# Batched matmul, 32 x (512 x 1024) x (1024 x 768): two outputs per store, the store moved behind the next x, and the first x cut into more pieces

## Chip, cores, metric

One core of one Trainium2 chip. The metric is device time of the slowest (here the only) core in microseconds, lower is better. A profiled execution is shown where traces are read; its span is some 1.5 to 2 us shorter than the time.

## The reference

```python
def setup_inputs():
    batch, m, k, n = 32, 512, 1024, 768
    return {"x": randn(batch, m, k).astype(float32), "weight": randn(batch, k, n).astype(float32)}

def reference(x, weight):
    return np.matmul(x, weight).astype(np.float32)
```

100.7 MB of weights, 67.1 MB of x and 50.3 MB of output pass between HBM and SBUF once each.

## The kernel before

The loads are issued by POOL and cast to bf16 on the way. x comes in pairs of batches (except the first and last), is transposed on PE, copied by DVE, multiplied against the weight, and evacuated by ACT and DVE to a float32 output tile.

```python
    AHEAD = 3; LATE = 4; HELD = 3
    w_pool   = ...tile_pool(name="w", bufs=4)
    x_pool   = ...tile_pool(name="x", bufs=3)
    out_pool = ...tile_pool(name="out", bufs=7)
    ...
    def load_pair(b):
        xs[b] = x_pool.tile([P, 2 * MT, K], BF16, name="x_sb")
        nc.gpsimd.dma_start(out=xs[b], in_=pair_view[b // 2])
    ...
    def evacuate(b, pair, pm):
        o = outs[b][:, pair * N2:(pair + 1) * N2]
        nc.scalar.copy(o[:, 0:512], pm[0])
        nc.vector.tensor_copy(o[:, 512:1024], pm[1])
        nc.scalar.copy(o[:, 1024:N2], pm[2])
    ...
        # first x: three of its four row tiles at once, the fourth in pieces
        x_fourth = out_pool.tile([P, 1, K], F32, name="out_sb")
        nc.sync.dma_start(x_first, x_view[0, :, :MT - 1])
        few = [slice(at, first + 20, 4) for first in (0, 20, 40) for at in range(first, first + 4)]
        for rows in (slice(64, P), slice(60, 64), *few):          # 64 rows, 4 rows, 12 times 5 rows
            nc.sync.dma_start(x_fourth[rows, 0], x_view[0, rows, MT - 1])
        load_w(0); ...; load_pair(1); load_w(1); load_w(2); load_pair(3)

        for b in range(B):
            if b % 2 and b + AHEAD + 1 < B:
                ...load_pair(b + AHEAD + 1)                       # (load_last for the last one)
            if b + AHEAD < B:
                load_w(b + AHEAD)
            if b <= B - LATE:
                if b > 0:
                    pending.append(b - 1)
                if b % 2 == 0 and b + AHEAD < B - HELD or b == B - LATE:
                    for at in pending:
                        nc.gpsimd.dma_start(out=out_view[at], in_=outs[at])
                    pending = []
            ...                                                   # the last four batches leave from SP
            outs[b] = out_pool.tile([P, MT * N], F32, name="out_sb")
            ...                                                   # transposes, matmuls, evacuate
```

Of the kernel before, what the change touches and what calls it, by code (L numbers as in the profile page):

```python
# [8 lines left out]
F32 = mybir.dt.float32  # L9
# [4 lines left out]
def kernel(  # L14
# [6 lines left out]
    nc = tc.nc  # L21
    B, M, K = x.shape
    _, _, N = weight.shape
    P = 128
    MT = M // P
# [4 lines left out]
    AHEAD = 3  # L30
    LATE = 4
    HELD = 3
# [2 lines left out]
    w_pool = ctx.enter_context(tc.tile_pool(name="w", bufs=4))  # L35
    x_pool = ctx.enter_context(tc.tile_pool(name="x", bufs=3))
    xT_pool = ctx.enter_context(tc.tile_pool(name="xT", bufs=6))
    out_pool = ctx.enter_context(tc.tile_pool(name="out", bufs=7))
    tpsum = ctx.enter_context(tc.tile_pool(name="tpsum", bufs=2, space=bass.MemoryType.PSUM))
    mpsum = ctx.enter_context(tc.tile_pool(name="mpsum", bufs=2, space=bass.MemoryType.PSUM))  # L40

# [4 lines left out]
    x_view = x.rearrange("b (mi mo) k -> b mi mo k", mi=P)  # L46
    pair_view = x[1:B - 1].rearrange("(p r) (mi mo) k -> p (r mi) mo k", r=2, mo=2 * MT)
    out_view = out.rearrange("b (mi mo) n -> b mi (mo n)", mi=P)

    xs, ws, outs = {}, {}, {}  # L50

    def banks():
        return [mpsum.tile([P, 512], F32, name=f"pm{i}") for i in range(3)]
# [6 lines that stand above are left out]
    def load_last():  # L60
        xs[B - 1] = x_pool.tile([P, MT, K], BF16, name="x_sb")
        nc.gpsimd.dma_start(out=xs[B - 1], in_=x_view[B - 1])  # L62

    def load_w(b):
        ws[b] = w_pool.tile([P, KT, N], BF16, name="w_sb")
        at = 0
        for n in CHUNKED.get(b, (KT,)):
            nc.gpsimd.dma_start(out=ws[b][:, at:at + n, :], in_=w_view[b, :, at:at + n, :])  # L68
            at += n
# [9 lines left out]
    def transpose_pair(b, mt):  # L79

        both = xT_pool.tile([P, 2, JT, P // 2, 2, 2], BF16, name="xT")
        for half in range(2):
            nc.vector.tensor_copy(  # L83
                both[:, :, :, :, half, :].rearrange("p b j i r -> p j b i r"),
                words(b, mt + MT * half).rearrange("p j (b i r) -> p j b i r", b=2, r=2),
            )
        return [both[:, r].rearrange("p j i h r -> p j (i h) r") for r in range(2)]

    def transpose_last(mt):
        xT = xT_pool.tile([P, JT, P, 2], BF16, name="xT")  # L90
        nc.vector.tensor_copy(  # L91
            xT.rearrange("p j m r -> p (j m r)"), words(B - 1, mt).rearrange("p j m -> p (j m)")
        )
        return xT

    def transpose_first(mt):

        xT = xT_pool.tile([P, JT, P, 2], BF16, name="xT")
        rows = x_first[:, mt] if mt < MT - 1 else x_fourth[:, 0]
        for h in range(2):  # L100
            pt = tpsum.tile([P, JT, P], F32, name="pt")
            for i in range(JT):
                nc.tensor.transpose(pt[:, i, :], rows[:, JT * h + i::KT], ident)  # L103
            nc.vector.tensor_copy(  # L104
                xT[:, 2 * h:2 * h + 2].rearrange("p j m r -> p j r m"),
                pt.rearrange("p (j r) m -> p j r m", r=2),
            )
        return xT
# [8 lines left out]
    def matmuls(pm, half, xT, b, kos, together):  # L117
        for ko in kos:
            for i, (bank, at, off, size) in enumerate(SPLITS[half]):
                shares = half == 1 and i == 0  # L120
                nc.tensor.matmul(  # L121
                    pm[bank][:, at:at + size],
                    xT[:, ko // 2, :, ko % 2],
                    ws[b][:, ko, off:off + size],
                    start=(ko == 0 and not (together and shares)),
                    stop=(ko == KT - 1),
                    skip_group_check=together,
                )

    def evacuate(b, pair, pm):  # L130
        o = outs[b][:, pair * N2:(pair + 1) * N2]
        nc.scalar.copy(o[:, 0:512], pm[0])  # L132
        nc.vector.tensor_copy(o[:, 512:1024], pm[1])  # L133
        nc.scalar.copy(o[:, 1024:N2], pm[2])  # L134

    with tc.manual_schedule():

        x_first = x_pool.tile([P, MT - 1, K], F32, name="x_sb")
        x_fourth = out_pool.tile([P, 1, K], F32, name="out_sb")
        nc.sync.dma_start(x_first, x_view[0, :, :MT - 1])  # L140
        few = [slice(at, first + 20, 4) for first in (0, 20, 40) for at in range(first, first + 4)]
        for rows in (slice(64, P), slice(60, 64), *few):
            nc.sync.dma_start(x_fourth[rows, 0], x_view[0, rows, MT - 1])
        load_w(0)
        ident = const.tile([P, P], F32)
        make_identity(nc, ident)
        load_pair(1)
        load_w(1)
        load_w(2)
        load_pair(3)  # L150

        ready = {}
        pending = []
        for b in range(B):
            if b % 2 and b + AHEAD + 1 < B:
                if b + AHEAD + 1 == B - 1:
                    load_last()
                else:
                    load_pair(b + AHEAD + 1)
            if b + AHEAD < B:  # L160
                load_w(b + AHEAD)
            if b <= B - LATE:
                if b > 0:
                    pending.append(b - 1)
                if b % 2 == 0 and b + AHEAD < B - HELD or b == B - LATE:
                    for at in pending:
                        nc.gpsimd.dma_start(out=out_view[at], in_=outs[at])  # L167
                    pending = []
            if b == B - 1:
                halves = [slice(pair * N2, (pair + 1) * N2) for pair in range(2)]  # L170
                nc.sync.dma_start(out_view[b - 1, :, halves[0]], outs[b - 1][:, halves[0]])
                for late in range(B - LATE, B - 2):
                    nc.sync.dma_start(out_view[late], outs[late])
                nc.sync.dma_start(out_view[b - 1, :, halves[1]], outs[b - 1][:, halves[1]])
            outs[b] = out_pool.tile([P, MT * N], F32, name="out_sb")
            if b == 0:
                xT = {mt: transpose_first(mt) for mt in range(MT - 1)}
            elif b == B - 1:
                xT = {mt: transpose_last(mt) for mt in range(MT)}
            else:  # L180
                if b % 2:
                    for mt in range(MT):
                        ready[b, mt], ready[b + 1, mt] = transpose_pair(b, mt)
                xT = {mt: ready.pop((b, mt)) for mt in range(MT)}
            if b not in CHUNKED:
                for pair in range(2):
                    pm = banks()
                    for half in range(2):
                        mt = 2 * pair + half
                        if mt not in xT:  # L190
                            xT[mt] = transpose_first(mt)
                        matmuls(pm, half, xT[mt], b, range(KT), False)
                    evacuate(b, pair, pm)
                continue
            pms = [banks() for _ in range(2)]
            at = 0
            for n in CHUNKED[b]:
                last = at + n == KT
                for mt in range(MT):
                    matmuls(pms[mt // 2], mt % 2, xT[mt], b, range(at, at + n), True)  # L200
                    if last and mt % 2 == 1:
                        pair = mt // 2
                        evacuate(b, pair, pms[pair])
                        if b == B - 1:
                            nc.sync.dma_start(out_view[b, :, halves[pair]], outs[b][:, halves[pair]])
                at += n
# [30 lines left out]
```

## Time and profile before

| | before |
|---|---|
| time, median of 3 runs | 515.02 us (515.02 to 515.08) |
| span of the profiled run | 513.6 us (a run of 515.37 us) |
| stores from POOL | 28 of 1536 KB |
| transfers that POOL issues per round of two batches | 5 |

A *round* below is two batches: one pair of x, two weights, two outputs. "Transfer engines" are the 16 DMA engines of the core. For each large transfer the trace has 16 landings, one per engine, without the engine's number; their spread shows how far the engines have drifted apart. These landings were read from the packed traces directly, so no printed view shows them. The *end* of a transfer is the 4-byte packet that each engine adds after its data (1296 on POOL's queue before, 16 for each of its 81 transfers).

### The profile page before, as it was taken

Reading aid. Unit: us, or ns where it says so; the run is one execution under the profiler, and the core shown is the slowest. Engines: PE = TensorE matmul, PEld = TensorE weight load, DVE = VectorE, ACT = ScalarE, POOL = GpSimd, SP = SyncE. Lnnn points to the kernel's source line nnn. Section 1 sums busy time; section 2 is a strip of 40 time slices with the busy share of each in tenths; the row PEclk is TensorE's granted clock in tenths of the full one; section 3 lists DMA queues with packets and bytes.
Section 4 is the critical chain, followed back from the end, with each engine's and each line's share of the span. In section 5 each row is a group of like instructions: output and inputs, shape, how many; then the busy total and the mean of one; then the engine's idle time right before and its main releaser. Section 6 shows DMA issues by size and latency. Waiting matters only on the chain.

```text
span 513.6 us, 5846 instructions
## 1 busy us (share of the span) xinstructions
PE 436.0 (85%) x2576; PEld 279.1 (54%) x2576; DVE 130.0 (25%) x196; ACT 76.2 (15%) x129; POOL 44.0 (9%) x87
## 2 busy tenths in 40 slices
PE   2808999999999798997979889898897989989990
PEld 1506666666666364654636546464563656656660
DVE  1205141323222141320414204141050422314120
ACT  0100211111111111111111111111111111110211
POOL 3000101001010101001010000100001101011000
PEclk9958999999999799998989979899897999999997
DMA  8999999999999999999999999999999999999997
GB/s 238 226 220 212 221 216 338 213 264 292 216 335 219 274 280 214 340 216 287 265 214 345 214 299 251 220 339 213 318 235 222 333 218 323 225 216 213 331 427 320
DMA packets 12904, 135.63 MB, mean 264 GB/s; under 512 B 1488, under 2 KB 1488, under 8 KB 3280
## 3 DMA queue, kind: packets, MB, share of 16 engines
q0 software_dynamic: 11664, 126.88, 96.5%
q1 hardware_dynamic: 1216, 8.39, 4.1%
q8 instruction: 20, 0.33, 0.2%
q14 instruction: 4, 0.03, 0.0%
HBM read 167.77 MB, written 50.33 MB: 425 GB/s over the span
## 4 chain that ended last, share of the span: by engine, by line
PE 39%; DMA 35%; issue 16%; DVE 4%; another core or an unknown queue 3%; POOL 1%; ACT 0%; POOLq 0%
PE pm L121 35%; DMA w_sb<-in_weight_dram 27%; DMA out_dram<-out_sb 6%; PE pt L76 4%; DVE xT L83 2%; DMA x_sb<-in_x_dram 2%; DVE out_sb L133 1%; POOL w_sb L68 0%; POOL x_sb L58 0%; POOL out_dram L167 0%; DVE xT L91 0%; ACT out_sb L134 0%; POOLq L167 0%; POOLq L68 0%
## 5 line engine op out<-in xcount | busy, mean ns | idle before, releaser
L121 PE MATMUL pm<-w_sb,xT 128*128 128x256 bf16 (+1 forms) x2048 | 354.0, 336 | 29.0 <-DMA w_sb<-in_weight_dram 29.0
L121 PEld LDWEIGHTS <-xT 128*128 128x128 bf16 x2048 | 205.3, 101 | 173.2 <-DMA w_sb<-in_weight_dram 32.8
L133 DVE COPY out_sb<-pm 128x512 f32<-128x512 f32 x64 | 44.3, 692 | 329.4 <-PE pm L121 306.1
L76 PE MATMUL pt<-ident,x_sb 128*128 128x128 f32 x496 | 79.7, 302 | 10.5 <-DVE xT L83 10.2
L76 PEld LDWEIGHTS pt<-ident,x_sb 128*128 128x128 f32 x496 | 69.2, 209 | 21.5 <-DVE xT L83 18.7
L83 DVE COPY xT<-pt 128x1024 bf16<-128x1024 bf16 x120 | 77.4, 687 | 11.0 <-PE pt L76 11.0
L132 ACT COPY out_sb<-pm 128x512 f32<-128x512 f32 x64 | 37.4, 585 | 282.3 <-PE pm L121 274.9
L134 ACT COPY out_sb<-pm 128x512 f32<-128x512 f32 x64 | 37.5, 586 | 143.4 <-PE pm L121 143.2
L68 POOL DMA_DIRECT2D w_sb<-in_weight_dram x37 | 19.8, 535 | 321.0 <-PE pm L121 307.7
L167 POOL DMA_DIRECT2D out_dram<-out_sb x28 | 15.0, 536 | 33.4 <-DMA w_sb<-in_weight_dram 25.4
L103 PE MATMUL pt<-ident,out_sb 128*128 128x128 f32 x8 | 1.9, 421 | 16.2 <-DMA out_sb<-in_x_dram 16.2
L103 PE MATMUL pt<-ident,x_sb 128*128 128x128 f32 x24 | 5.8, 422 | 10.2 <-DMA x_sb<-in_x_dram 10.2
L104 DVE CAST xT<-pt 128x512 bf16<-128x512 f32 x8 | 5.9, 732 | 31.9 <-PE pt L103 31.4
L58 POOL DMA_DIRECT2D x_sb<-in_x_dram x15 | 8.1, 540 | 67.0 <-DMA w_sb<-in_weight_dram 55.8
L103 PEld LDWEIGHTS pt<-ident,out_sb 128*128 128x128 f32 x8 | 1.6, 218 | 16.5 <-issue 16.5
L103 PEld LDWEIGHTS pt<-ident,x_sb 128*128 128x128 f32 x24 | 4.4, 214 | 11.2 <-issue 10.2
L91 DVE COPY xT<-pt 128x1024 bf16<-128x1024 bf16 x4 | 2.6, 686 | 0.2 <-PE pt L76 0.2
L132 ACT ACT_TABLE_LOAD x1 | 1.3, 1283 | 0.7 <-PEq L221 0.7
L62 POOL DMA_DIRECT2D x_sb<-in_x_dram x1 | 0.5, 527 | 6.8 <-DMA w_sb<-in_weight_dram 6.8
masks.py:199 POOL TENSOR_SCALAR_AFFINE_SELECT ident<-ident 128x128 f32<-128x128 f32 x1 | 0.3, 287 | 0.1
masks.py:197 POOL MEMSET ident<- 128x128 f32 x1 | 0.2, 223 | 0.0
L221 POOL MEMSET const-float32-0.0<- 128x1 f32 x1 | 0.1, 98 | 0.2 <-issue 0.2
(3 smaller groups left out, 0.3 us busy)
## 6 DMA issues: line engine op xcount, KB each, us to landing
w_sb<-in_weight_dram POOLq DMA_DIRECT2D x28, 1536.0 KB, 41.9
out_dram<-out_sb POOLq DMA_DIRECT2D x28, 1536.0 KB, 44.7
x_sb<-in_x_dram POOLq DMA_DIRECT2D x15, 2048.0 KB, 48.3
w_sb<-in_weight_dram POOLq DMA_DIRECT2D x7, 768.0 KB, 37.0
out_dram<-out_sb SPq DMA_DIRECT2D x4, 768.0 KB
out_dram<-out_sb SPq DMA_DIRECT2D x2, 1536.0 KB
x_sb<-in_x_dram SPq DMA_DIRECT2D x1, 1536.0 KB
x_sb<-in_x_dram POOLq DMA_DIRECT2D x1, 1024.0 KB, 36.2
```

The costliest lines, as they stand in the source:

```text
L58: nc.gpsimd.dma_start(out=xs[b], in_=pair_view[b // 2])
L68: nc.gpsimd.dma_start(out=ws[b][:, at:at + n, :], in_=w_view[b, :, at:at + n, :])
L76: nc.tensor.transpose(pt[:, j, :], pairs[:, mo, j::JT], ident)
L83: nc.vector.tensor_copy(both[:, :, :, :, half, :].rearrange("p b j i r -> p j b i r"), words(b, mt + MT * half).rearrange("p j (b i r) -> ...
L91: nc.vector.tensor_copy(xT.rearrange("p j m r -> p (j m r)"), words(B - 1, mt).rearrange("p j m -> p (j m)"))
L103: nc.tensor.transpose(pt[:, i, :], rows[:, JT * h + i::KT], ident)
L104: nc.vector.tensor_copy(xT[:, 2 * h:2 * h + 2].rearrange("p j m r -> p j r m"), pt.rearrange("p (j r) m -> p j r m", r=2),)
L121: nc.tensor.matmul(pm[bank][:, at:at + size], xT[:, ko // 2, :, ko % 2], ws[b][:, ko, off:off + size], start=(ko == 0 and not (together an ...
L132: nc.scalar.copy(o[:, 0:512], pm[0])
L133: nc.vector.tensor_copy(o[:, 512:1024], pm[1])
L134: nc.scalar.copy(o[:, 1024:N2], pm[2])
L167: nc.gpsimd.dma_start(out=out_view[at], in_=outs[at])
```

## The change

The intent is fewer and larger stores and an x load that no longer stands behind stores. The order in POOL's queue goes from "weight, store, store, x, weight" to "weight, x, store pair, weight". The buffers follow (three pairs and a single for seven singles), and the first x goes in three more pieces.

```diff
-    out_pool = ctx.enter_context(tc.tile_pool(name="out", bufs=7))
+    out_pool = ctx.enter_context(tc.tile_pool(name="out", bufs=3))
+    one_pool = ctx.enter_context(tc.tile_pool(name="one", bufs=1))
...
+    two_view = out.rearrange("(p r) (mi mo) n -> p mi r (mo n)", r=2, mi=P)
...
+    def open_out(b):
+        if b == B - 2:
+            outs[b] = one_pool.tile([P, MT * N], F32, name="one_sb")
+            return
+        if b % 2 == 0 or b == B - 1:
+            twos[b // 2] = out_pool.tile([P, 2, MT * N], F32, name="out_sb")
+        outs[b] = twos[b // 2][:, b % 2]
...
-        x_fourth = out_pool.tile([P, 1, K], F32, name="out_sb")
+        x_fourth = one_pool.tile([P, 1, K], F32, name="one_sb")
...
-        for rows in (slice(64, P), slice(60, 64), *few):
+        for rows in (slice(64, 96), slice(96, 112), slice(112, P), slice(60, 62), slice(62, 64), *few):
...
+        def store(at):
+            nc.gpsimd.dma_start(out=two_view[at], in_=twos[at])
...
+            if b % 2 and 2 < b < B - HELD - AHEAD:
+                store((b - 3) // 2)
             if b + AHEAD < B:
                 load_w(b + AHEAD)
-            if b <= B - LATE:
-                ... (pending and its stores, shown above)
+            if b == B - LATE:
+                store(b // 2 - 2)
+                store(b // 2 - 1)
```

More of the change, by code (lines that the diff above doesn't have):

```diff
@@ L48 @@
     out_view = out.rearrange("b (mi mo) n -> b mi (mo n)", mi=P)
-    xs, ws, outs = {}, {}, {}
+    two_view = out.rearrange("(p r) (mi mo) n -> p mi r (mo n)", r=2, mi=P)
+    xs, ws, outs, twos = {}, {}, {}, {}
     def banks():
@@ L150 @@
         load_pair(3)
+        def store(at):
+            nc.gpsimd.dma_start(out=two_view[at], in_=twos[at])
         ready = {}
-        pending = []
         for b in range(B):
@@ L159 @@
                     load_pair(b + AHEAD + 1)
+            if b % 2 and 2 < b < B - HELD - AHEAD:
+                store((b - 3) // 2)
             if b + AHEAD < B:
                 load_w(b + AHEAD)
-            if b <= B - LATE:
-                if b > 0:
-                    pending.append(b - 1)
-                if b % 2 == 0 and b + AHEAD < B - HELD or b == B - LATE:
-                    for at in pending:
-                        nc.gpsimd.dma_start(out=out_view[at], in_=outs[at])
-                    pending = []
+            if b == B - LATE:
+                store(b // 2 - 2)
+                store(b // 2 - 1)
             if b == B - 1:
@@ L174 @@
                 nc.sync.dma_start(out_view[b - 1, :, halves[1]], outs[b - 1][:, halves[1]])
-            outs[b] = out_pool.tile([P, MT * N], F32, name="out_sb")
+            open_out(b)
             if b == 0:
```

## The prediction

> **What bounds the kernel now.** I read the page's slices and queues first, because the page says at once whether an engine or the transfers are full; then the totals of waits, the chain of waits, and the stretches around the end.
>
> ```profile
> span 513.6 us, 5846 instructions
> PE 436.0 (85%) x2576; PEld 279.1 (54%) x2576; DVE 130.0 (25%) x196; ACT 76.2 (15%) x129; POOL 44.0 (9%) x87
> ...
> DMA  8999999999999999999999999999999999999997
> ...
> q0 software_dynamic: 11664, 126.88, 96.5%
> q1 hardware_dynamic: 1216, 8.39, 4.1%
> ...
> HBM read 167.77 MB, written 50.33 MB: 425 GB/s over the span
> ```
>
> The DMA row has nines from the second slice to the next to last, and the two data queues add up to 100.6% of 16 engines' time (packets overlap a little). The bytes on the HBM side are 167.77 + 50.33 = 218.1 MB. No engine of the core is that full: PE is busy 85% and waits in every round once it has caught up. So this is a transfer stream that never runs dry, and the time is its length plus a head and a tail.
>
> The chain of waits gives the length of one round (two batches: one pair of x, two weights, two outputs). These are the ends of the same step, one round apart:
>
> ```profile
> 246.71 0.68 DVE xT L83
> ...
> 262.25 3.37 another core or an unknown queue
> ...
> 278.09 0.69 DVE xT L83
> ...
> 310.91 0.68 DVE xT L83
> ...
> 341.56 0.68 DVE xT L83
> ...
> 373.44 0.69 DVE xT L83
> ```
>
> (373.44 - 246.71) / 4 = 31.68 us a round. A round moves 2 x 2.097 (x) + 2 x 3.146 (weights) + 2 x 1.573 (outputs) = 13.63 MB on the HBM side, so 430 GB/s. The "unknown queue" of 3.37 us in each round is PE waiting for the second weight of the round: PE has some 3 us of slack a round.
>
> Is the stream ever close to running dry? The waits of the issuing engine:
>
> ```profile
> POOL w_sb L68 <- PE pm L121: 307.7, 27, 28.7
> ...
> POOL x_sb L58 <- DMA w_sb<-in_weight_dram: 55.8, 9, 6.6
> ...
> PE pt L103 <- DMA out_sb<-in_x_dram: 16.2, 1, 16.2
> ...
> POOL out_dram L167 <- DMA w_sb<-in_weight_dram: 25.4, 10, 3.5
> ```
>
> POOL waits 307.7 us for PE to free a weight buffer, yet a transfer lands a median 41.9 us (weights), 44.7 us (outputs) and 48.3 us (x) after its issue. So there is well over a round of work queued. I compared every issue with the landing of the transfer ahead of it, as the trace records them: the least reserve is 11.4 us, at the weight issued at 61.6 us, and later it is 30 to 40 us.
>
> The end, as stretches of time (the last two columns are the DMA share and GB/s) and in order of time:
>
> ```profile
> 496.00:504.00 8.00, 5.92 (x37) 3.32 (x35) 1.38 (x2) 2.30 (x4) 0.00 (x0) 1.00 1.01 431
> 504.00:512.00 8.00, 0.00 (x0) 0.00 (x0) 0.00 (x0) 0.00 (x0) 0.00 (x0) 0.71 0.80 336
> ```
> ```profile
> 501.27 1.63 SPq L205 DMA_DIRECT2D out_dram<-out_sb  x2
> ...
> 501.96 0.59 ACT L134 COPY out_sb<-pm 128x512 f32<-128x512 f32 x1 [0.17 <-PE pm L121]
> ```
>
> The arithmetic ends at 502.55 us, the transfers run on to about 512. The last store waits behind queued stores and not behind arithmetic. In the trace the 16 engines finish that store between 509.2 and 512.45 us (mean 511.1): the slowest engine sets the end, and perfect balance would be worth about 1.4 us.
>
> **What the Trainium skill says.** DMA: Bandwidth & Descriptors, section "Where 436 GB/s comes from", puts the fabric ceiling at 435.2 GB/s. The trace agrees with a limit there: a round runs at 430. By that figure a round could not be shorter than 13.63 MB / 435.2 = 31.32 us (an estimate), so only 0.36 us a round is left for anything that reorders or merges transfers. The same page, "Rules for kernel authors", advises at least 1 MiB per DMA and coalescing of small ones; these stores are 1.5 MiB already. Its section "Anatomy of one DMA" calls the semaphore write at the end of a transfer almost free and the fixed cost a matter of completion latency. The trace agrees: with the queue full, that latency is beside other data. Its section "Queues, rings and completion order" says that an engine takes turns between the queues that have work, a packet each. The trace agrees in the first 40 us, as worked out below.
>
> **The change part by part.**
>
> *Merged stores.* 28 stores on POOL become 14 of twice the size. Bytes and rows stay: 12 KB rows, 8 rows per engine and batch. What goes is 14 transfer ends. I size an end by the steps between the last landings of successive weight transfers in the trace: a full weight takes 7.28 us, half of one 3.66, a quarter 1.85 (1.87 and 1.83). 3.66 - 1.85 = 1.81 us is the pure data of a quarter, so 0.04 us is left per transfer; 2 x 3.66 - 7.28 gives 0.04 too. The gain is 14 x 0.04 = 0.56 us, on the path, as all 16 engines are full. Upper bound: if all of the 0.36 us a round were per transfer, one in five of them would be 0.07 us, and 14 of them 1.0 us.
>
> *Order.* Before: weight, store, store, x, weight. After: weight, x, store pair, weight. It is the same batches that are stored; x only passes ahead of them. A round still has one run of stores between loads, so I count no gain and no loss. "One pair older" refers to the place in the loop: what was stored at the top of batch 2 is stored at the top of batch 3, still ahead of batch 3's weight.
>
> *Waits on transfer counters.* In the built program each POOL transfer waits for the one eight before it. At five a round that is 1.6 rounds, and it is the 55.8 and 25.4 us of waits on weights above; at four a round it is two full rounds, and those waits should all but vanish. This is off the path: it moves issues a few us earlier into a queue holding 30 to 40 us of work.
>
> *Output buffers.* Seven single ones become three pairs and one single. Pair p+3 may be written when store p has landed. In the queue, store p stands ahead of the weight that batch 2p+6 needs before it can compute, so the store lands first. No wait.
>
> *First x.* 64 rows in one transfer become 32 + 16 + 16, still four rows on each engine. Four rows (one on each of four engines) become 2 + 2 (by the trace's landings of such small transfers, one engine per row). I expect engines 0 and 1 to get one row of 4 KB more and engines 2 and 3 one less: 4096 B at 430/16 = 26.9 GB/s is 0.15 us. If the slowest engine is one of the first two, the end comes 0.15 us later; if it is one of the next two, 0.15 us earlier. The added ends cost at most 3 x 0.04 = 0.12 us. The fourth tile of x lands later: on an engine that serves both queues the parts after the first take about 31 turns between 10.1 us (the first x there) and 39.97 us (PE goes on), 0.96 us a turn; four more turns put it near 44 us. PE is then 4 us late, and the least reserve falls from 11.4 us to about 7.5. It still doesn't run dry, and PE makes up 4 us from its 3 us a round of slack.
>
> Sum: -0.56 (ends) + 0.1 (added ends) +/- 0.15 (rows) = about -0.4 us. 515.02 - 0.4 = **514.6 us**.
>
> **The rivals.**
>
> *The stream runs dry early.* For it: x lands later, PE starts later, and PE frees the weights. Against it: 11.4 us of reserve against 4. If the tile came 15 us late, the loss would be 15 - 11.4 = some 4 us: 518 to 519.
>
> *Deeper issue pays.* If the 81 us of waits on older transfers starved the engines, removing them would show. Against it: the DMA share is never under 0.97 in any 8 us stretch between the first and the last. At the ceiling of the skill's page, all 16 rounds would give 16 x 0.36 = 5.8 us: 509.3. I give that little.
>
> *Output buffers held longer become a wait.* A pair is freed as a whole and the store lands some 10 us later, behind x. Should ACT or DVE wait 1 to 2 us a round for a buffer, PE's 3 us of slack would hide it; only above that would it lengthen rounds, 1 us each being 16 us, or 531. The order in the queue speaks against it.
>
> *Imbalance of the engines.* Their finish differs by 3.2 us. Instruction fetches fall on single engines (16 KB in about 0.9 us in the trace), and a shifted fetch can make another engine the last. That is worth up to 0.7 us either way, more than my central gain.
>
> **Range and chances.** The gain has a hard top of about 1.0 us from the ends plus 0.7 from balance, while the same 0.7 and 0.15 can be lost: 513.6 to 515.5 holds the outcomes in which no new wait appears, and those I give over 8 in 10. Two per cent is 10.3 us; nothing short of the third rival in full reaches it on the slow side, and the ceiling forbids it on the fast side: 0.005 faster, 0.98 within, 0.015 slower.
>
> **What would show it.** Right: still nines in the DMA row; a round of 31.6 to 31.7 us in the chain; POOL's waits on weights near zero and its waits on PE longer; 14 store issues of 3072 KB; PE going on with the fourth tile near 44 us; no ACT or DVE wait on a store. Wrong: a DMA digit under 9 between 60 and 100 us (dry early), a wait of ACT or DVE for a store (buffers), or a round clearly under 31.5 us (the steps between landings hid a larger cost per transfer).

## The result

| | before | changed |
|---|---|---|
| median of 4 runs | 515.05 us (515.02 to 515.28) | 514.59 us (514.4 to 515.2) |
| repeated: 9 and 5 runs on one chip | 514.97 us (514.86 to 515.09) | 514.57 us (514.50 to 514.81) |
| span of the profiled run | 513.6 us (a run of 515.37 us) | 512.7 us (a run of 514.44 us) |
| store lands after issue, median | 44.7 us (1536 KB) | 55.3 us (3072 KB) |

Ratios are the mean time of one kernel's fast runs over that of the other's of the same rounds, so not quite the ratio of the medians. They are 0.9992 (95% interval 0.9975 to 1.0009) and, repeated, 0.9993 (0.998 to 1.0005). Both intervals contain 1. In the repeat, though, no run of the changed kernel is as slow as the fastest run of before (514.81 against 514.86). So I take a gain of about 0.4 us as likely, and tell below what it is made of as far as differences of 0.1 to 0.3 us can be told. Most differences below are of 0.2 to 0.4 us between medians of five runs; by the spread of those runs each is uncertain by 0.1 to 0.25 us.

The page of the changed kernel, first its slices and queues:

```profile
span 512.7 us, 5785 instructions
...
DMA  8999999999999999999999999999999999999998
...
q0 software_dynamic: 11440, 126.88, 96.6%
q1 hardware_dynamic: 1248, 8.39, 4.1%
...
HBM read 167.77 MB, written 50.33 MB: 425 GB/s over the span
```

The same bytes, and still nines from the second slice to the next to last: the stream of transfers sets the time as before. The queue of POOL has 224 packets fewer (11664 before): 14 ends on each of 16 engines.

The totals of waits (engine, line, what it waited for: us in total, times, longest):

```profile
POOL w_sb L70 <- PE pm L123: 397.6, 28, 32.9
...
PE pt L105 <- DMA one_sb<-in_x_dram: 19.1, 1, 19.1
...
POOL x_sb L60 <- DMA w_sb<-in_weight_dram: 10.9, 1, 10.9
...
POOL w_sb L70 <- DMA w_sb<-in_weight_dram: 2.2, 1, 2.2
POOL x_sb L64 <- DMA w_sb<-in_weight_dram: 2.1, 1, 2.1
```

POOL's waits on older weights fell from 93.4 us (55.8 + 25.4 + 6.8 + 5.4) to 15.2 (10.9 + 2.2 + 2.1; the 10.9 is one wait at the start, which the page of before puts down to PE with 11.2), and its wait for PE grew from 307.7 to 397.6. Over 75 us of waiting were exchanged for other waiting, and the time moved by 0.4 us. No ACT or DVE wait on a store appears.

The chain of waits, the same step of each round as shown for before, here seven rounds apart:

```profile
214.72 0.69 DVE xT L85
...
436.39 0.69 DVE xT L85
```

(436.39 - 214.72) / 7 = 31.67 us a round, against 31.68 before. The rounds are as long as they were.

The start in order of time, two lines of before and then the changed kernel: PE's fourth tile, and the issue of the two weights and of the first store:

```profile
39.97 1.94 PE L103 MATMUL pt<-ident,out_sb 128*128 128x128 f32 x8 [16.18 <-DMA out_sb<-in_x_dram]
...
61.62 0.53 POOL L68 DMA_DIRECT2D w_sb<-in_weight_dram  x1 [15.55 <-PE pm L121]
```
```profile
42.90 1.94 PE L105 MATMUL pt<-ident,one_sb 128*128 128x128 f32 x8 [19.08 <-DMA one_sb<-in_x_dram]
...
49.52 0.53 POOL L70 DMA_DIRECT2D w_sb<-in_weight_dram  x1 [32.95 <-PE pm L123]
...
65.60 0.53 POOL L70 DMA_DIRECT2D w_sb<-in_weight_dram  x1 [15.55 <-PE pm L123]
66.12 0.54 POOL L60 DMA_DIRECT2D x_sb<-in_x_dram  x1
66.64 0.72 POOL L164 DMA_DIRECT2D out_dram<-out_sb  x1
```

PE is 2.9 us later than before (39.97), and the weight of 61.62 us now goes out at 65.60. By the trace the weight ahead of it starts landing 7.4 us later, so that is the reserve that is left. The stream never empties. And the end, in stretches (the last two columns are DMA share and GB/s):

```profile
496.00:504.00 8.00, 5.81 (x36) 3.24 (x34) 1.38 (x2) 2.30 (x4) 0.00 (x0) 1.00 1.00 422
504.00:512.00 8.00, 0.00 (x0) 0.00 (x0) 0.00 (x0) 0.00 (x0) 0.00 (x0) 0.60 0.79 330
```

As before, the last 8 us are transfers alone. By the trace, the 16 engines land the last store between 509.09 and 511.74 us (mean 510.72), against 509.22 to 512.45 (mean 510.91) before. The slowest engine gained 0.71 us, the mean 0.19. (The mean of 511.1 in the prediction, and the 0.27 and 1.34 us in two expectations below, take the last 16 landings of all, some of which belong to the store before; this document takes the last store's own.) That is one execution each, and they are 0.93 us apart in time (515.37 and 514.44) where the medians are 0.46 apart, so the 0.71 overstates the gain.

### The profile page after: what moved, and what is told of

The parts are those of the page before. It is cut to its first block, busy times and chain, and to the rows that moved or that the text cites. A ratio compares the mean times of both kernels' runs of the same rounds, so it can differ in the third digit from the quotient of the medians.

```text
span 512.7 us, 5785 instructions
## 1 busy us (share of the span) xinstructions
PE 435.4 (85%) x2576; PEld 278.7 (54%) x2576; DVE 130.0 (25%) x196; ACT 76.1 (15%) x129; POOL 39.1 (8%) x73
## 2 busy tenths in 40 slices
DMA packets 12712, 135.63 MB, mean 265 GB/s; under 512 B 1296, under 2 KB 1296, under 8 KB 3088
## 4 chain that ended last, share of the span: by engine, by line
PE 46%; DMA 37%; issue 8%; DVE 5%; another core or an unknown queue 1%; POOL 1%; ACT 0%; SPq 0%; POOLq 0%
PE pm L123 40%; DMA w_sb<-in_weight_dram 28%; DMA one_sb<-in_x_dram 8%; PE pt L78 5%; DVE xT L85 4%; DVE out_sb L144 1%; POOL out_dram L164 0%; PE pt L105 0%; POOL w_sb L70 0%; POOL x_sb L60 0%; DVE one_sb L144 0%; DVE xT L93 0%; ACT out_sb L145 0%; SPq L151 0%
## 5 line engine op out<-in xcount | busy, mean ns | idle before, releaser
L144 DVE COPY out_sb<-pm 128x512 f32<-128x512 f32 x62 | 42.9, 691 | 317.6 <-PE pm L123 317.6
L143 ACT COPY out_sb<-pm 128x512 f32<-128x512 f32 x62 | 36.3, 585 | 271.7 <-PE pm L123 271.7
L145 ACT COPY out_sb<-pm 128x512 f32<-128x512 f32 x62 | 36.3, 585 | 145.7 <-PE pm L123 145.6
L70 POOL DMA_DIRECT2D w_sb<-in_weight_dram x37 | 20.1, 544 | 404.8 <-PE pm L123 397.6
L105 PE MATMUL pt<-ident,one_sb 128*128 128x128 f32 x8 | 1.9, 421 | 19.1 <-DMA one_sb<-in_x_dram 19.1
L105 PEld LDWEIGHTS pt<-ident,one_sb 128*128 128x128 f32 x8 | 1.6, 219 | 19.4 <-issue 19.4
L164 POOL DMA_DIRECT2D out_dram<-out_sb x14 | 10.1, 719 | 6.7 <-ACT out_sb L143 3.5
L105 PEld LDWEIGHTS pt<-ident,x_sb 128*128 128x128 f32 x24 | 4.1, 209 | 11.5 <-issue 10.3
L60 POOL DMA_DIRECT2D x_sb<-in_x_dram x15 | 8.1, 539 | 10.9 <-DMA w_sb<-in_weight_dram 10.9
L144 DVE COPY one_sb<-pm 128x512 f32<-128x512 f32 x2 | 1.4, 690 | 9.0 <-PE pm L123 9.0
L143 ACT COPY one_sb<-pm 128x512 f32<-128x512 f32 x2 | 1.2, 585 | 6.4 <-PE pm L123 6.4
L145 ACT COPY one_sb<-pm 128x512 f32<-128x512 f32 x2 | 1.2, 585 | 1.6 <-PE pm L123 1.6
## 6 DMA issues: line engine op xcount, KB each, us to landing
out_dram<-out_sb POOLq DMA_DIRECT2D x14, 3072.0 KB, 55.3
```

Source lines behind the costliest of these rows:

```text
L70: nc.gpsimd.dma_start(out=ws[b][:, at:at + n, :], in_=w_view[b, :, at:at + n, :])
L105: nc.tensor.transpose(pt[:, i, :], rows[:, JT * h + i::KT], ident)
L164: nc.gpsimd.dma_start(out=two_view[at], in_=twos[at])
```

## The experiments

Theory: the gain is small because the stream is full; it consists of fewer transfer ends and of a better balance of the engines. Rivals: only one of the two; or the order or the buffers; or chance. Then two questions on what might have gone wrong: how much lateness of PE and how much less buffer the reserve can take.

### The parts, one at a time (one chip, 5 runs each; before 514.97 us, 514.86 to 515.09)

The changed kernel again.

> The changed kernel again, for a tighter interval. Its profile showed the 16 transfer engines end 0.27 us earlier in the mean and 0.71 us earlier for the slowest. Theory (ends of transfers plus balance of the engines): 0.3 to 0.7 us faster than before. Rival (noise of the balance alone, nothing gained): 0 within 0.2 us.

514.57 us (514.50 to 514.81): -0.40 us, in the expected range.

The changed kernel with the old pieces of the first x:

```diff
-        for rows in (slice(64, 96), slice(96, 112), slice(112, P), slice(60, 62), slice(62, 64), *few):
+        for rows in (slice(64, P), slice(60, 64), *few):
```

> The changed kernel with the first x in its old pieces. If merging the stores is the gain, it keeps 0.3 to 0.5 us of it and the slowest engine ends within 0.2 us of the changed kernel's. If the new pieces of the first x give the gain by balancing the engines, it falls back to before within 0.15 us. PE goes on with the fourth tile at 40 us.

514.78 us (514.72 to 514.79): -0.19, between the two outcomes that were laid down. The stores, the order and the buffers together do not have the whole gain.

The kernel before with the new pieces (the same line, the other way):

> The kernel before with only the first x in the new pieces. Theory of balance: 0.2 to 0.4 us faster than before, the slowest engine ends nearer to the mean (under 1.0 us over it, from 1.34). Rival (only the merging counts): equal to before within 0.15 us. PE goes on with the fourth tile near 43 us.

514.71 us (514.59 to 515.02): -0.26. The expected 0.2 to 0.4 came, but not its sign in the trace: the slowest engine was 1.46 us over the mean of the last store (512.29 against 510.82), hardly less than the 1.54 of before. But the profile is of the slowest of the five runs (515.02 us), so it says little of the median. The two parts add up within the noise: -0.19 - 0.26 = -0.45 against -0.40 for both.

The changed kernel with each pair stored by two transfers:

```diff
-            nc.gpsimd.dma_start(out=two_view[at], in_=twos[at])
+            for r in range(2):
+                nc.gpsimd.dma_start(out=out_view[2 * at + r], in_=twos[at][:, r])
```

> The changed kernel with each pair stored by two transfers again, everything else as changed. If a transfer's end costs 0.04 us, it is 0.56 us slower than the changed kernel; if 0.02 us, 0.28 us slower; if order and buffers give the gain, equal to the changed kernel. The waits of the issuing engine on older weights return (some 80 us in total).

514.86 us (514.66 to 515.08): 0.29 slower than the changed kernel (uncertain by 0.2), 0.02 us per end if all of it is ends. The waits on older weights are back, 47.2 + 10.8 + 6.8 + 6.2 = 71.0 us (the 10.8 is again the one at the start), and waits and ends together cost no more than these 0.29 us. This kernel differs from the previous one by order and buffers alone, and is 0.15 us slower, within the spread of its runs: they gain nothing that shows.

### What a transfer's end costs

First try: four transfers for each pair, cut by batch and by halves of the partitions.

```diff
-            nc.gpsimd.dma_start(out=two_view[at], in_=twos[at])
+            for r in range(2):
+                for part in (slice(0, 64), slice(64, P)):
+                    nc.gpsimd.dma_start(out=out_view[2 * at + r, part], in_=twos[at][part, r])
```

> The changed kernel with each pair stored by four transfers (one batch, half of the partitions each): the same rows and bytes, 56 transfers for 14. At 0.02 us per end (what the runs so far give: 14 ends, about 0.3 us) it is 0.84 us slower than the changed kernel, 515.4 us; at the predicted 0.04 us, 1.7 us, 516.3 us; if ends cost nothing, 514.6 us. The issuing engine waits on older transfers again, but the queue does not run dry.

527.73 us (525.33 to 528.93), 12.7 over before: none of the three. By the trace the engines are 6.8 us apart when the seventh weight lands (2.4 in the changed kernel) and land the last store 8.5 us apart; the mean landing of the last store is 9.7 us later than the changed kernel's. So this cut slows the stream itself, and not evenly: in the mean, the last three of the four transfers of the first pair land some 2.4 us apart, and the gap between the engines opens there. Most of those in the middle rounds land 1.84 us apart, which is as fast as the full stores of before (3.66 us each). The last four are slow again, 2.0 to 3.5 us apart. The kernel also has fewer partitions per transfer, so it does not measure ends, and two cleaner runs followed. Why half of the partitions costs so much, and why at the two ends of the run, was not settled.

Second try: all 128 partitions, rows of 6 KB, once in 28 and once in 56 transfers.

```diff
-            nc.gpsimd.dma_start(out=two_view[at], in_=twos[at])
+            for h in (slice(0, N2), slice(N2, 2 * N2)):                       # 28 transfers
+                nc.gpsimd.dma_start(out=two_view[at][:, :, h], in_=twos[at][:, :, h])
```
```diff
+            for r in range(2):                                                # 56 transfers
+                for h in (slice(0, N2), slice(N2, 2 * N2)):
+                    nc.gpsimd.dma_start(out=two_view[at][:, r, h], in_=twos[at][:, r, h])
```

> The changed kernel with each pair's store cut by columns into two transfers with rows of 6 KB on all 128 partitions: 28 transfers. To be read against the next run, which has the same rows in 56. By the profile a 6 KB row takes 234 ns and a 12 KB row 460, so twice the rows cost 8 ns each on 224 more rows per engine, 1.8 us; with 14 more ends at 0.02 us, 0.3 us: 516.7 us.

> The same 6 KB rows in 56 transfers, one batch and half of its columns each. At 0.02 us per end 0.56 us slower than the run with 28, at 0.04 us 1.1 us slower; if an end costs nothing, equal. If it is 5 us or more slower, ends cost far more than thought and the 12.7 us of the store by halves of the partitions was ends too; if not, that was the split of the partitions.

516.31 us (516.08 to 516.51) and 516.60 us (516.43 to 516.87), before 515.08 on that chip. The difference of 0.29 us over 28 ends is **0.010 us per end**, half of the lower figure expected and a quarter of the predicted one. The two ranges touch, and the 0.29 is uncertain by 0.25, so 0 to 0.02 us per end are possible; 0.04, which would be 1.1 us, is not. The 12.7 us of the first try were therefore not ends. Rows do cost. The 28 transfers are 1.23 us over before and the changed kernel is 0.40 under it on its chip, 1.63 us between them; less 14 ends at 0.01 that is 1.5 us for 224 more rows per engine, 6.6 ns a row, near the 8 ns worked out beforehand from the packets' durations.

### The balance of the engines

Only the move of rows, without the cut of the 64 rows, in the kernel before:

```diff
-        for rows in (slice(64, P), slice(60, 64), *few):
+        for rows in (slice(64, P), slice(60, 62), slice(62, 64), *few):
```

> The kernel before with only the four rows of the first x in two transfers of two (rows moved from the third and fourth engine to the first two), the 64 rows in one transfer. If the balance of rows is what the new first x gains, this has its 0.2 to 0.3 us over before (514.7 us); if the split of the 64 rows does it (other turns between the queues), equal to before (515.0 us).

514.81 us (514.75 to 514.93), before 515.08 (514.76 to 515.31): -0.27 (uncertain by 0.15), as much as the whole new first x gave on the other chip. So it is the four rows in two transfers; of the cut of the 64 no effect shows. The move was meant to matter by one row of 4 KB, 0.15 us; it gives up to twice that. In this one profile the last landing is 511.94 us against 512.45, and the slowest engine is 1.17 us over the mean, against 1.54.

The fourth tile spread evenly, eight rows on each engine:

```diff
-        for rows in (slice(64, 96), slice(96, 112), slice(112, P), slice(60, 62), slice(62, 64), *few):
+        for rows in (slice(0, P),):
```

> The changed kernel with the fourth tile of the first x in one transfer of 128 rows: eight rows on each engine instead of up to 18 on five of them and four on the rest. PE goes on with the fourth tile by 16 us instead of 43. If the uneven start sets the end (the five are the last at the end), 0.8 to 1.2 us faster than the changed kernel. If it is a counterweight (the other engines are slowed by some 0.6 us each by instruction fetches later), within 0.3 us of it, with other engines last.

516.18 us (515.83 to 516.35): 1.2 us slower than before, outside both outcomes and on the far side of the second. PE was not held up at all; it came to the fourth tile at 23.5 us, when it was done with the tiles before. What happened instead stands in the landings. When the second weight lands, at 33.6 us, 15 of the 16 engines are within 0.5 us of each other; by 484 us six are still within 0.35 us and the others have fallen behind by up to 4.6 us; the slowest lands the last store at 513.48 us (511.74 in the changed kernel). In the changed kernel five engines start 1.6 to 1.9 us behind the first (at 33.7 us), and by 482 us the whole spread is 2.7. So the lopsided start is a **counterweight**: the engines that take fewer rows at the start lose time later. The sum of the work is the same: from the second to the last weight the mean landing moves by 448.79 us here and by 448.73 in the changed kernel.

What takes that time can be seen in part. The trace has 20 instruction fetches of 16 KB, 0.88 to 0.98 us each on one engine. In the changed kernel eleven of the engines land within 0.6 us at 39 us. After one fetch ten of them still do, after two nine, and so on one for one down to three after eight fetches, at 199 us; the five engines with more rows stay the last, and the whole spread stays at 2.4 to 2.9 us. The profiles of before, of the changed kernel again and of both halves of the change show the same count. So a fetch sets the engine that it falls on back by 0.6 to 0.9 us, and the first eight fall on engines with fewer rows. In the level kernel nothing stands against that. Fetches are not all of it: between the second and the last weight the engines' lateness behind the first of them, summed over the 16, grows by 27.2 us there, and the 18 fetches in that time took 16.8.

Half way between:

```diff
-        few = [slice(at, first + 20, 4) for first in (0, 20, 40) for at in range(first, first + 4)]
+        few = [slice(at, 20, 4) for at in range(4)] + [slice(20, 30, 2), slice(21, 30, 2)]
-        for rows in (slice(64, 96), slice(96, 112), slice(112, P), slice(60, 62), slice(62, 64), *few):
+        for rows in (slice(64, P), slice(32, 64), slice(30, 32), *few):
```

> The changed kernel with the fourth tile spread half way: six rows on each engine from two transfers, and the other 32 on the first five (12 to 13 rows there against 16 to 18 in the changed kernel and 8 with all level). If the counterweight acts in proportion, the mean of changed (514.6) and level (516.2): 515.3 to 515.5 us. If the best balance lies between them, under 514.4 us, which would beat both kernels. PE goes on with the fourth tile near 28 us.

515.16 us (515.01 to 515.39), near the proportional 515.3 to 515.5 and not under 514.4. Three points, 8, 12 to 13 and 16 to 18 rows on the five engines, give 516.2, 515.2 and 514.6 us. More rows there help as far as tried, and the next experiment shows what stops it. PE went on at 31.7 us.

### How close the start is to running dry

```diff
-        few = [slice(at, first + 20, 4) for first in (0, 20, 40) for at in range(first, first + 4)]
+        few = [slice(at, first + 12, 4) for first in range(0, 60, 12) for at in range(first, first + 4)]
```

> The changed kernel with the 60 rows in 20 transfers of three rows instead of 12 of five: eight more rows and 16 more turns on the first three engines, so PE goes on some 16 us later, near 59 us. If the reserve of 7.4 us is real, the queue runs dry for some 8 us between 75 and 84 us and the time is 521 to 524 us. If PE's start never matters, only the 1.2 us of rows on three engines: 515.5 to 516.5 us.

528.2 us (527.55 to 528.7): 13.6 us over the changed kernel, so dry, and more so than expected. In the stretches of this kernel (next to last column the DMA share):

```profile
64.00:72.00 8.00, 7.28 (x47) 5.72 (x46) 5.84 (x9) 0.59 (x1) 0.53 (x1) 1.00 0.88 172
72.00:80.00 8.00, 7.95 (x51) 4.87 (x51) 0.69 (x1) 1.76 (x3) 0.00 (x0) 1.00 0.37 78
80.00:88.00 8.00, 8.00 (x50) 4.79 (x50) 1.38 (x2) 1.76 (x3) 1.76 (x3) 1.00 0.65 122
88.00:96.00 8.00, 7.46 (x49) 5.58 (x47) 3.65 (x6) 1.17 (x2) 0.56 (x1) 1.00 0.98 208
```

against the changed kernel in the same stretches:

```profile
64.00:72.00 8.00, 8.00 (x52) 4.78 (x50) 1.38 (x2) 1.75 (x3) 1.76 (x3) 1.00 0.99 209
72.00:80.00 8.00, 7.35 (x48) 5.37 (x45) 3.99 (x7) 1.17 (x2) 0.56 (x1) 1.00 1.03 219
80.00:88.00 8.00, 7.97 (x50) 5.22 (x51) 2.55 (x4) 1.17 (x2) 0.00 (x0) 1.00 1.04 221
```

PE went on at 60.00 us, 17.1 us after the changed kernel. The weights went out at 65.88 and 81.94 us, and the transfers ahead of them had begun to land 0.2 and 6.6 us before that. The second found all engines idle and landed 9.5 to 10.4 us after its issue, 2.3 to 3.1 us more than the 7.3 of its data: an empty queue pays the lead-in that a full one hides. The mean landing of the seventh weight is 11.5 us later than in the changed kernel (117.11 against 105.66), and nothing later gives it back. The rest of the 13.6 is balance: three engines have eight rows more, and the slowest engine lands the last store 2.7 us over the mean, against 1.0. So the 11.5 us are the loss that the 7.4 us of reserve holds off. The rival "PE's start never matters" is out.

### How close the output buffers are

```diff
-    out_pool = ctx.enter_context(tc.tile_pool(name="out", bufs=3))
+    out_pool = ctx.enter_context(tc.tile_pool(name="out", bufs=2))
```

> The changed kernel with two pairs of output buffers instead of three. Now a pair may be written only when the store that stands 24 us behind its weight has landed: ACT and DVE wait for stores in every round. If the queue's reserve of 30 to 40 us takes this up, the time stays within 1 us of the changed kernel and only the reserve shrinks, to some 10 us; if not, 16 rounds lengthen by 1 us or more each: over 530 us.

538.52 us (537.82 to 539.09). The waits are there, 13 each, once a round:

```profile
DVE out_sb L144 <- DMA out_dram<-out_sb: 180.2, 13, 23.2
ACT out_sb L143 <- DMA out_dram<-out_sb: 178.5, 13, 23.1
```

The time lies in the second outcome, but by neither mechanism that was laid down. The rounds did not lengthen: the last weight lands at 482.9 us (482.4 in the changed kernel). Look at the end of this kernel (busy us of PE first, then weight loads, DVE, ACT, POOL, clock, DMA share, GB/s):

```profile
472.00:488.00 16.00, 5.88 (x38) 3.89 (x37) 0.00 (x0) 0.00 (x0) 0.00 (x0) 0.84 1.03 313
488.00:504.00 16.00, 11.63 (x63) 8.13 (x65) 6.64 (x10) 2.05 (x4) 0.00 (x0) 0.74 0.46 196
504.00:520.00 16.00, 15.60 (x98) 9.90 (x99) 3.75 (x6) 4.69 (x8) 0.00 (x0) 1.00 0.18 74
520.00:536.00 16.00, 11.41 (x70) 7.07 (x71) 2.98 (x5) 2.30 (x4) 0.00 (x0) 0.94 0.78 321
```

against the changed kernel:

```profile
488.00:504.00 16.00, 13.51 (x85) 8.72 (x83) 4.64 (x7) 2.91 (x6) 0.00 (x0) 1.00 1.01 429
```

All loads are in by 483 us and the transfers then wait for PE, which runs late by the wait for a store (23 us at its longest). In the middle the queue hides that lateness entirely; it is paid once, at the end, where nothing is left to hide it: 23.9 us over the changed kernel, about one such wait.

## Why the prediction was right, point by point

- **The bound.** Right. A full DMA row before and after, and rounds of 31.68 and 31.67 us.
- **The sum.** 514.6 us predicted, 514.59 and 514.57 measured. But two of its terms were mis-sized, and the errors cancelled: that the sum fits so closely is luck.
- **Merged stores, -0.56 us.** Too large. Taken out alone they are worth 0.29 us; the cleaner pair of runs gives 0.010 us per end, so 0.15 us for 14. The two do not differ beyond their noise, and both exclude 0.56. The step that failed is the 0.04 us per transfer, taken from landing steps of weights of three sizes. A remainder of 0.04 out of steps of 1.8 to 7.3 us was finer than that method carries.
- **First x, +/- 0.15 us and up to +0.12.** Its part was -0.26 and -0.27 us in two kernels: the more favourable of the two signs offered, and larger. Shown: the move of rows gives as much without the cut of the 64 rows. Not shown: which engines were last; the trace does not number them, and the expected narrowing of the spread came in one of the two profiles (1.17 us over the mean) and not in the other (1.46, of a slow run).
- **Order and buffers, 0.** Right within the noise: +0.15 us, uncertain by more than that.
- **Waits on older transfers, off the path.** Right. They fell by 78 us, returned to 71 in the run with single stores, and neither moved the time by more than the 0.3 to 0.4 us that the merging may explain as well.
- **PE near 44 us, reserve 7.5 us.** 42.90 us and 7.4. A turn of the two queues is thus 0.73 us here (2.93 us for four turns), not 0.96. The late-x experiment shows that the reserve is real. (Its "later 30 to 40 us" holds for the middle only: the same reading gives 16 us at 88 us and 19 to 24 us from 450 us on.)
- **The ceiling.** Not shown. The figure of 435.2 GB/s belongs to SBUF's ports, and the loads reach SBUF as bf16: the trace counts 135.63 MB and a mean of 264 GB/s there. The 430 GB/s of a round count the bytes in HBM. That the two figures are close does not show that this ceiling sets the 31.68 us, so 31.32 us as the least is open; the two profiles gave 31.68 and 31.67.
- **The rivals.** "Dry early" was put at 4 us for a tile 15 us later. The experiment, 17.1 us later than the changed kernel, lost 13.6 us: less reserve to start from (7.4 us, as the changed kernel has already used 4), the lead-in of a queue that has run empty, and some 2 us of balance. "Output buffers" was sized as 1 us a round, 16 times; with one pair fewer it is one lateness of PE, paid once at the end. "Imbalance" was right in naming a size (0.7 us) as large as the gain, and wrong in treating it as chance: the kernel's odd first pieces set it, against fetches whose first eight leave the same pattern in five profiles.

## What to carry to other kernels

When the transfer engines are full from end to end, waits of the issuing engine are worth little (here 78 us of them went for at most 0.4 us), and a merge of transfers that are already megabytes is worth only the ends it saves, here 0.01 to 0.02 us each. The remaining microsecond is in how evenly the transfer engines finish, and levelling the start need not level the finish: measure the finish. Before taking buffers or lead away from such a kernel, compute the least reserve in the queue, and look at the end for lateness that the middle hides.

## What the Trainium skill lacked or had wrong

- DMA: Bandwidth & Descriptors, "Anatomy of one DMA": its fixed cost of about 2.0 us per DMA is not to be added up in a full queue. The runs show 0.010 us per end (28 more ends, 0.29 us, uncertain by 0.25). Where the queue had run empty, 2.3 to 3.1 us came on top of the data.
- The same page, "Rules for kernel authors", says that transfers on disjoint partition halves serialize and not to bother. It does not say that in a full stream it can cost: storing by halves of the partitions took 527.73 us against 514.57, engines up to 6.8 us apart at the first stores, of which ends explain about 0.4 us (42 at 0.010). SBUF — State Buffer gives a single transfer on half of the partitions fewer ports and a lower rate, but that is not the pattern here: most of these halves landed 1.84 us apart, the full rate.
- The same page as the first, "Queues, rings and completion order", gives the turns between queues at packet granularity. It does not give a duration: here four more turns on an engine delayed a small transfer by 2.93 us beside loads of 24 to 32 KB rows.
- That page calls two of the 16 engines usually slower than the rest, without a size. No page that I read tells that evenly loaded engines finish unevenly by several us over 500 us, nor that a deliberate imbalance at the start pays: 516.18 us level, 515.16 half way, 514.57 lopsided.
- Runtime: NRT & Kernel Launch, "Instruction fetch mechanics", calls the cost of a 16 KiB fetch mostly hidden. It does not say what a fetch costs the data beside it: here about 0.9 us on one engine, after which that engine's data land 0.6 to 0.9 us later. The rest of the drift was not settled.
